# Gate rows of a chunked recurrence: loaded once and spread by VectorE shuffles, in place of repeated broadcast loads

## The chip, the cores and the metric

The kernel runs on one core of one Trainium2 chip. The metric is the device time of one execution in microseconds, from runs on the chip. The profile is one more execution, recorded by the hardware profiler.

The engines that matter here: TensorE (PE, matmuls, with PEld for its weight loads), VectorE (DVE), ScalarE (ACT), GpSimd (POOL), and SyncE (SP), which only issues transfers. Transfers between DRAM and the on-chip memory run on 16 DMA engines that all queues share. Each engine works through its own instructions in a fixed order and waits on semaphores for the others.

## The reference, cut to what matters

One encoder layer over 2048 positions of width 1024, in float32: a combined input projection, a Hyena group (long convolutions by FFT, 512 channels) beside an mLSTM group (4 heads of 128), an output projection, cross-attention into 256 memory positions, an MLP, and RMS norms between them. The change is in the mLSTM group, a recurrence over chunks, run once in each direction:

```python
F = jnp.cumsum(fc, axis=-1)
logw = F[..., :, None] - F[..., None, :] + ic[..., None, :]
logw = jnp.where(lower, logw, -jnp.inf)
log_inter = F + m[..., None]
m_t = jnp.maximum(log_inter, jnp.max(logw, axis=-1))
w = jnp.exp(logw - m_t[..., None])
inter = jnp.exp(log_inter - m_t)
s = jnp.einsum('bhtd,bhsd->bhts', qc, kc) * w
num = jnp.einsum('bhts,bhse->bhte', s, vc) + inter[..., None] * jnp.einsum('bhtd,bhde->bhte', qc, C)
den = jnp.sum(s, axis=-1) + inter * jnp.einsum('bhtd,bhd->bht', qc, n)
h = num / jnp.maximum(jnp.abs(den), jnp.exp(-m_t))[..., None]
```

For each chunk, head and direction two vectors over the position t are needed: the negated running maximum (less the gate sum), which goes into the exponent of `w`, and `inter`, which scales the queries that meet the carried state.

## The kernel before, in words

The kernel works in chunks of 128 positions, so 16 chunks, with both directions handled together. The scores are held transposed, key position s in the partitions and query position t along the columns, four heads of 128 side by side: tiles of 128 x 512.

`gates` (lines 961 to 1060) computes the gate vectors of all chunks once, with (direction, chunk, head) as 128 rows and the 128 positions as columns, and stores two such tables to DRAM as `rows` (lines 1046 and 1047): `rows[0]` holds the negated maxima, `rows[1]` the factors `inter`. Since t runs along the columns of the score tiles, a chunk's row has to stand in all 128 partitions alike. The kernel before gets that from the transfer itself: for each chunk, direction and kind one load (line 1159) reads four rows of 128 numbers, 2 KB, and writes them to each of the 128 partitions of a tile `rw`, 256 KB. Chunk 0 forward and chunk 15 backward need no `inter`, so there are 62 such loads.

`mlstm` (line 1114) is the stage around them. It first runs the rest of the backward states (`backward`, line 1096: loads `kn` and `va`, a product on POOL, matmuls L1081, updates on VectorE L1087, stores to `cbd`). Then `loads(n)` (line 1140) issues the loads of chunk n: queries `qn`, keys `kk_t`, backward state `cbn`, values `va`, and the rows. It is called for chunks 0 and 1 ahead of the loop, and for chunk n + 2 at the end of chunk n. `rw` has four buffers for each kind, so the tiles of chunk n + 2 reuse those of chunk n. The loads of chunks 0 and 1 are pinned to the written order of the program (`keep_in_program_order`), except for `va`.

`scores(n)` computes the key-query products (L1168), multiplies the `inter` rows by the queries on POOL (L1174), adds the causal mask to the maxima on POOL (L1175), takes the exponential on ScalarE (L1177), and multiplies by the products on VectorE (L1178). The loop then forms numerator and denominator on TensorE (L1206 with the values, L1208 with the carried state), the absolute value on ScalarE (L1211), `den` on VectorE (L1214, L1215), the output `y` (tile `ht`, L1219 and L1223, two buffers), the update of the forward state (L1077, L1081, L1087), the output gate on POOL (L1228), squares on ScalarE (L1234), and after every second chunk an inverse root (lines 206 to 218), the normalisation (L1241) and the stores to `ym` (L1243).

The stage is not alone. It is interleaved by generators (`weave`, `take`) with the memory projections before it and with the attention stage behind it, whose first block of 512 positions reads four chunks of `ym`. In both, weights are loaded by SP (L368, L373, L1268), split into a high and a low part by ScalarE and VectorE (L344), and used in matmuls of three parts (L339, L340, L341). A scheduler then puts each engine's instructions in order by a modelled timeline, except for what is pinned. A change in one stage can therefore move instructions of the others.

Of the kernel before, what the change touches and what calls it, by code (L numbers as in the profile page):

```python
# [10 lines left out]
F32 = mybir.dt.float32  # L11
# [122 lines left out]
class Prog:  # L134
# [931 lines left out]
    def load_v(self, sb, n):  # L1066
        t = sb.tile([128, 4, 129], F32, tag="va", name="va", bufs=2)
        vd = self.dram("vd", (L, CH)).rearrange("(n s) c -> s n c", s=128)
        self.nc.sync.dma_start(out=t[:, :, 0:128], in_=vd[:, n].rearrange("s (h d) -> s h d", h=4))
        self.nc.vector.memset(t[:, :, 128:129], 1.0)  # L1070
        return t
# [42 lines left out]
    def mlstm(self, es):  # L1114
        nc, tc, a = self.nc, self.tc, self.a
# [5 lines left out]
        rows = self.dram("rows", (2, 128, 128))  # L1121
        cbd = self.dram("cbd", (15, 128, 516))
        sb = es.enter_context(tc.tile_pool(name="m_sb", bufs=1, side="right"))
# [4 lines left out]
        for d in range(2):  # L1128
            m = sb.tile([128, 128], F32, name=f"mask{d}")
            nc.gpsimd.memset(m, 0.0)  # L1130
            s = 1 if d == 0 else -1
            nc.gpsimd.affine_select(m, m, pattern=[[s, 128]], compare_op=ALU.is_ge, fill=-1.0e30,
                                    base=0, channel_multiplier=-s)
            masks.append(m)

        for _ in self.backward(sb, 7, 0, self.old_state(sb, 8)):
            yield 3
        load, load_v, update = (partial(f, sb) for f in (self.load_c, self.load_v, self.update))

        def loads(n):  # L1140
            get = (lambda out, in_: tc.keep_in_program_order(nc.sync.dma_start(out=out, in_=in_))) if n < 2 else \
                (lambda out, in_: nc.sync.dma_start(out=out, in_=in_))
            qn = sb.tile([128, 4, 128], F32, tag="qn", name="qn", bufs=2)
            kk_t = sb.tile([128, 4, 128], F32, tag="kt", name="kk_t", bufs=2)
            get(out=qn, in_=qt[:, :, 128 * n:128 * n + 128])
            get(out=kk_t, in_=kt_[:, :, 128 * n:128 * n + 128])
            cbn = None
            if n < 15:
                cbn = sb.tile([128, 4, 129], F32, tag="cbn", name="cbn", bufs=2)
                get(out=cbn.rearrange("d h e -> d (h e)"), in_=cbd[n])  # L1150
            va = load_v(n)
            rows_ = {}
            for d in range(2):
                r = 64 * d + 4 * n
                for i in range(2):
                    if i == 1 and (n == 0, cbn is None)[d]:
                        continue
                    t = sb.tile([128, 4, 128], F32, tag=f"r{i}", name="rw", bufs=4)
                    get(out=t.rearrange("p h t -> p (h t)"),
                                      in_=rows[i, r:r + 4].rearrange("h t -> (h t)").unsqueeze(0).broadcast_to([128, 512]))  # L1160
                    rows_[d, i] = t
            return qn, kk_t, cbn, va, rows_

        def scores(n, ld):
# [4 lines left out]
            for d in range(2):  # L1169
# [8 lines left out]
                nc.vector.tensor_tensor(nm, nm, sp, ALU.mult)  # L1178

        ld, stores = [loads(0), loads(1)], []  # L1180
        scores(0, ld[0])
        cf = None
        for n in range(16):
# [10 lines left out]
            for d in range(2):  # L1194
                r = 64 * d + 4 * n
# [5 lines left out]
                for p in range(2):  # L1201
                    pn = self.hy()
                    for i in range(2):
                        h = 2 * p + i
# [11 lines left out]
                for p, pv in enumerate(pvs):  # L1216
# [4 lines left out]
                    for i in range(2):  # L1221
                        h = 2 * p + i
# [13 lines left out]
            if n % 2:  # L1236
                rv = self.bank_rsqrt(sb, ss, 128)
                for i, y in enumerate(ys):
                    t0 = 128 * (n - 1 + i)
                    for h in range(4):  # L1240
# [3 lines left out]
                        out=ym[t0:t0 + 128].rearrange("t (h e) -> t h e", h=4), in_=y))  # L1244
            if n < 14:
                ld.append(loads(n + 2))
# [713 lines left out]
```

## Time and profile before

| what | value |
|---|---|
| median of three runs | 3217.77 us (3217.51 to 3219.89) |
| profiled execution | 3216.99 us |
| its span, first to last instruction | 3215.3 us |
| mean granted TensorE clock | 0.981 |
| PE busy | 3047.5 us, 95% |
| DVE busy | 2036.0 us, 63% |
| ACT busy | 1500.1 us, 47% |
| POOL busy | 1182.7 us, 37% |
| moved by DMA | 617.87 MB, mean 192 GB/s |

How to read the lines below: a group of instructions is named by its line in the kernel (L1178 is line 1178), its engine and operation, what it writes and what it reads (`rw<-rows`), and its shapes. "Idle before" is the time in which the engine stood still just ahead of these instructions, with what ended most of it. The chain of waits is followed back from the last instruction, at each step to what released it. The granted clock is the share of TensorE's full clock that it was given. The recurrence's chunks run from about 1190 to 1640 us of the span.

### The profile page before, as it was taken

Reading aid. Unit: us, or ns where it says so; the run is one execution under the profiler, and the core shown is the slowest. Engines: PE = TensorE matmul, PEld = TensorE weight load, DVE = VectorE, ACT = ScalarE, POOL = GpSimd, SP = SyncE. Lnnn points to the kernel's source line nnn. Section 1 sums busy time; section 2 is a strip of 40 time slices with the busy share of each in tenths; the row PEclk is TensorE's granted clock in tenths of the full one; section 3 lists DMA queues with packets and bytes.
Section 4 is the critical chain, followed back from the end, with each engine's and each line's share of the span. In section 5 each row is a group of like instructions: output and inputs, shape, how many; then the busy total and the mean of one; then the engine's idle time right before and its main releaser. Section 6 shows DMA issues by size and latency. Waiting matters only on the chain.

```text
span 3215.3 us, 43642 instructions
## 1 busy us (share of the span) xinstructions
PE 3047.5 (95%) x14473; PEld 2394.2 (74%) x14473; DVE 2036.0 (63%) x3439; ACT 1500.1 (47%) x2873; POOL 1182.7 (37%) x818
## 2 busy tenths in 40 slices
PE   6999999999999976999999998999999999999998
PEld 4655566876668765878887886888788878888876
DVE  7775366345865755667775547556645676556595
ACT  5533366434764343454444445455555443333335
POOL 0122012100121334224151217776756483434483
PEclk9999999999999997999999999999999999999999
DMA  5564776686687989657484537665644474444434
GB/s 189 191 206 162 247 201 202 178 274 185 180 235 209 295 281 280 195 174 246 141 276 141 182 111 243 215 198 179 201 152 153 157 246 154 144 129 150 125 92 167
DMA packets 453817, 617.87 MB, mean 192 GB/s; under 512 B 39630, under 2 KB 251726, under 8 KB 452568
## 3 DMA queue, kind: packets, MB, share of 16 engines
q1 hardware_dynamic: 415412, 556.57, 55.2%
q10 hardware_dynamic: 38180, 58.51, 5.5%
q8 instruction: 115, 1.88, 0.2%
q14 instruction: 110, 0.90, 0.1%
HBM read 416.73 MB, written 198.21 MB: 191 GB/s over the span
## 4 chain that ended last, share of the span: by engine, by line
PE 71%; DMA 13%; DVE 8%; issue 3%; ACT 3%; POOL 1%; SPq 1%; ACTq 0%; DVEq 0%; POOLq 0%
PE mm L339 15%; PE mm L341 15%; PE mm L340 15%; PE hy L341 5%; PE hy L339 5%; PE hy L340 5%; PE hy L176 2%; DMA rw<-rows 2%; PE hy L875 1%; PE mm L844 1%; PE hy L917 1%; DVE wl L344 1%; DMA xt<-in_x_t_dram 1%; DVE bl L1533 1%; DMA va<-vd 1%
## 5 line engine op out<-in xcount | busy, mean ns | idle before, releaser
L344 DVE TENSOR_TENSOR wl<-wn,wh 128x512 fp32r<-128x512 f32 (+1 forms) x364 | 289.0, 829 | 125.5 <-ACT wh L344 124.9
L1533 DVE TENSOR_TENSOR bl<-wr,bh 128x512 fp32r<-128x512 f32 x213 | 241.1, 1138 | 126.8 <-ACT bh L1532 123.2
L1532 ACT CAST ah<-w 128x512 fp32r<-128x512 f32 x284 | 176.3, 622 | 300.1 <-PE hy L340 154.8
L344 ACT CAST wh<-wn 128x512 fp32r<-128x512 f32 (+1 forms) x364 | 207.9, 618 | 209.3 <-PE mm L341 47.8
L922 POOL TENSOR_TENSOR b<-b,a 128x512 f32<-128x512 f32 x64 | 87.7, 1370 | 581.4 <-ACT b L920 457.1
L339 PE MATMUL mm<-xh,wh 128*128 128x512 f32 x640 | 270.1, 423 | 4.5 <-ACT xh L499 2.3
L1533 DVE TENSOR_TENSOR al<-w,ah 128x512 fp32r<-128x512 f32 x236 | 222.0, 942 | 58.6 <-ACT ah L1532 58.6
L340 PE MATMUL mm<-xl,wh 128*128 128x512 f32 x640 | 256.7, 402 | 1.9 <-DVE xl L344 1.4
L341 PE MATMUL mm<-xh,wl 128*128 128x512 f32 x640 | 258.1, 404 | 0.0
L1532 ACT CAST bh<-wr 128x512 fp32r<-128x512 f32 x232 | 143.7, 621 | 240.0 <-PE mm L341 177.0
L341 PE MATMUL mm<-bh,al 128*128 128x512 f32 x576 | 225.4, 394 | 8.0 <-DVE al L1533 4.7
L339 PE MATMUL mm<-bh,ah 128*128 128x512 f32 x576 | 226.6, 393 | 0.1
L340 PE MATMUL mm<-bl,ah 128*128 128x512 f32 x576 | 225.8, 392 | 0.0
L339 PE MATMUL mm<-act,wh 128*128 128x512 f32 x512 | 199.0, 394 | 4.2 <-ACT act L344 2.7
L340 PE MATMUL mm<-act,wh 128*128 128x512 f32 x512 | 201.2, 394 | 0.0
L341 PE MATMUL mm<-act,wl 128*128 128x512 f32 x512 | 200.0, 392 | 0.3 <-DVE wl L344 0.3
L1382 POOL TENSOR_TENSOR ssum<-ssum,sq 128x512 f32<-128x512 f32 x56 | 81.1, 1448 | 287.7 <-ACT sq L1381 287.7
L339 PE MATMUL hy<-bh,ah 128*128 128x512 f32 x448 | 175.2, 391 | 0.0
L340 PE MATMUL hy<-bl,ah 128*128 128x512 f32 x448 | 174.6, 390 | 0.0
L341 PE MATMUL hy<-bh,al 128*128 128x512 f32 x448 | 174.4, 390 | 0.0
L339 PEld LDWEIGHTS mm<-xh,wh 128*128 128x128 f32 x640 | 121.1, 189 | 65.4 <-issue 29.5
L339 PE MATMUL hy<-xh,ah 128*128 128x512 f32 x384 | 152.2, 397 | 8.9 <-ACT ah L1532 8.2
(367 smaller groups left out, 8439.4 us busy)
## 6 DMA issues: line engine op xcount, KB each, us to landing
wr<-hc SPq DMA_DIRECT2D x224, 256.0 KB
w<-in_ff_w_dram SPq DMA_DIRECT2D x176, 256.0 KB
hc<-t SPq DMA_DIRECT2D x128, 256.0 KB
wn<-in_w_in_dram SPq DMA_DIRECT2D x100, 256.0 KB
hc<-q SPq DMA_DIRECT2D x96, 256.0 KB
fs<-a SPq DMA_DIRECT2D x32, 512.0 KB
a<-fs SPq DMA_DIRECT2D x64, 256.0 KB
a<-zs SPq DMA_DIRECT2D x64, 256.0 KB
```

Of the source, the lines that this page charges most:

```text
L176: b = self.nc.tensor.matmul(*products[-1], start=True, stop=True)
L339: mm(ps, lh, rh, start=start, stop=False)
L340: mm(ps, lh, rl, start=False, stop=False)
L341: mm(ps, ll, rh, start=False, stop=stop)
L344: both = (self.nc.scalar.copy(hi, src), self.nc.vector.tensor_tensor(lo, src, hi.bitcast(F32), ALU.subtract))
L844: nc.tensor.matmul(pp, dm[:, m], t[:, m], start=True, stop=True)
L875: nc.tensor.matmul(pg, em[:, m], y, start=True, stop=True)
L917: nc.tensor.matmul(pp, dm[:, m], t[:, m], start=True, stop=True)
L922: nc.gpsimd.tensor_tensor(xt, xt, hi[:, m], ALU.mult)
L1382: nc.gpsimd.tensor_tensor(ssum, ssum, sq, ALU.add)
L1532: self.nc.scalar.copy(hi, src)
L1533: eng.tensor_tensor(lo, src, hi.bitcast(F32), ALU.subtract)
```

## The change

In place of the 62 broadcast loads, the tables are loaded once into two tiles `rows0` and `rows1`, each 128 x 512. Tile s holds the rows of chunks 8s to 8s + 7, for both directions and both kinds: 2 x 2 x 8 = 32 rows of 512 numbers (four heads of 128), one to a partition. A VectorE shuffle moves data among the 32 partitions of a group only, so the same 32 rows are loaded four times, one copy to each group of 32 partitions: eight loads of 64 KB, ahead of the remaining backward states. Where `loads(n)` issued a row load on SP, it now issues a `stream_shuffle` on VectorE, whose mask names one partition for all 32 outputs: each group of 32 partitions fills with one row, and so all 128. The tiles `rw`, their number of buffers and all that reads them stay as they are. The shuffles are not pinned for chunks 0 and 1, as the loads were.

```diff
+        packed_rows = []
+        by_half = rows.rearrange("i (d s n h) t -> s (i d) n (h t)", d=2, s=2, n=8)
+        for s in range(2):
+            t = sb.tile([128, 512], F32, name=f"rows{s}")
+            for q in range(4):
+                nc.sync.dma_start(out=t[32 * q:32 * q + 32], in_=by_half[s])
+            packed_rows.append(t)
         for _ in self.backward(sb, 7, 0, self.old_state(sb, 8)):
             yield 3
...
             for d in range(2):
-                r = 64 * d + 4 * n
                 for i in range(2):
                     if i == 1 and (n == 0, cbn is None)[d]:
                         continue
                     t = sb.tile([128, 4, 128], F32, tag=f"r{i}", name="rw", bufs=4)
-                    get(out=t.rearrange("p h t -> p (h t)"),
-                                      in_=rows[i, r:r + 4].rearrange("h t -> (h t)").unsqueeze(0).broadcast_to([128, 512]))
+                    nc.vector.stream_shuffle(out=t.rearrange("p h t -> p (h t)"), in_=packed_rows[n // 8],
+                                             mask=[16 * i + 8 * d + n % 8] * 32)
                     rows_[d, i] = t
```

## The prediction, made before the result was known

> **What bounds the kernel now.** First the page's header, then the busy time of the engines by stretch (columns: PE, PEld, DVE, ACT and POOL busy with counts, granted clock, DMA share, GB/s).
>
> ```profile
> span 3215.3 us, 43642 instructions
> ```
>
> ```profile
> 1150.00:1185.00 35.00, 27.39 (x152) 22.50 (x151) 16.32 (x46) 11.41 (x21) 7.61 (x11) 0.95 0.99 311
> 1185.00:1300.00 115.00, 78.19 (x443) 68.72 (x444) 64.11 (x187) 49.40 (x171) 49.50 (x38) 0.81 0.93 288
> 1300.00:1625.00 325.00, 314.97 (x1670) 267.30 (x1669) 226.54 (x538) 156.01 (x425) 89.30 (x65) 0.99 0.58 184
> 1625.00:3215.00 1590.00, 1546.62 (x6863) 1272.93 (x6861) 1007.70 (x1350) 715.09 (x1282) 840.40 (x572) 0.99 0.53 170
> ```
>
> TensorE sets the pace nearly everywhere (97% busy from 1300 us on). The exception is 1150 to 1300 us: there the DMA engines are 93 to 99% busy, TensorE idles 44 us (7.6 and 36.8) and its clock falls to 0.81. That is where the recurrence starts, and the chain of waits through it, next, says on what.
>
> ```profile
> by line: DMA rw<-rows 32.0%; issue 10.8%; PE hy L1206 5.5%; POOL rw L1175 5.4%; DVE ht L1241 5.2%; DMA qn<-qt 5.1%; PE hy L1081 4.6%; DMA va<-vd 4.6%; ACT rw L1177 4.0%; PE hy L1208 3.7%; PE hy L1168 3.2%; PE hy L1343 2.1%; PE mm L339 1.7%;
> ...
> 1187.33 6.31 DMA rw<-rows
> 1193.65 7.97 DMA rw<-rows
> ...
> 1212.68 6.93 DMA rw<-rows
> ...
> 1227.91 5.65 DMA rw<-rows
> ...
> 1260.37 5.37 DMA rw<-rows
> ...
> 1284.40 6.14 DMA qn<-qt
> 1290.57 6.22 DMA rw<-rows
> ```
>
> This view covers 1185 to 1305 us, 120 us. Row loads hold 32% of it: the six rows sum to 38.4 us. How many loads that is, by the issues of 1185 to 1300 us and by the tile over the whole run:
>
> ```profile
> DMA packets 30429, 33.17 MB, mean 288 GB/s; under 512 B 1923, under 2 KB 19866, under 8 KB 30419
> ...
> rw<-rows SPq DMA_DIRECT2D x31, 256.0 KB
> ```
>
> ```profile
> L1142 SPq DMA_DIRECT2D rw<-rows x55: 319/423/1635, 1195.1 to 1560.4; - x55
> L1141 SPq DMA_DIRECT2D rw<-rows x7: 319/423/611, 1185.0 to 1194.3; - x7
> ```
>
> So 62 loads of 256 KB in all, 31 of them (8.13 MB of 33.17) in the bound stretch.
>
> **What the change removes.** Sixty-two loads go. Were the stretch set by DMA throughput alone, 8.13 MB at 288 GB/s is 28 us; the chain gives 38 us as the upper end. Neither is paid in full, because something else is late next each time, so I walk the places, taking TensorE's gaps with the rows that end them (in brackets: idle before, releaser).
>
> ```profile
> 1237.17 0.77 PE L1206 MATMUL hy<-va,rw 128*128 128x129 f32 x2 [5.12 <-issue]
> ...
> 1251.01 2.06 PE L1081 MATMUL hy<-ve,kn 128*128 128x129 f32 x8 [8.84 <-issue]
> ```
>
> ```profile
> 1271.14 0.77 PE L1206 MATMUL hy<-va,rw 128*128 128x129 f32 x2 [7.18 <-issue]
> ```
>
> ```profile
> 1198.87 0.70 SPq L1141 DMA_DIRECT2D qn<-qt  x1
> ...
> 1238.71 2.17 SPq L1370 DMA_DIRECT2D acc<-in_x_t_dram  x1
> 1240.97 1.37 SPq L1142 DMA_DIRECT2D rw<-rows  x1
> 1242.44 1.08 SPq L1243 DMA_DIRECT2D ym<-ht  x1
> 1243.62 0.58 SPq L1142 DMA_DIRECT2D rw<-rows  x1
> ```
>
> ```profile
> 1264.40 1.26 POOL L1228 TENSOR_TENSOR ht<-ht,og 128x512 f32<-128x512 f32 x1
> 1265.90 1.43 POOL L1175 TENSOR_TENSOR rw<-rw,mask 128x512 f32<-128x512 f32 x1 [0.24 <-DMA rw<-rows]
> ```
>
> - Start: the chain's first 14.3 us (1187.33 to 1201.62) are row loads. Next late is `qn`, issued at 1198.87, behind eight row loads (seven by L1141, the first by L1142): 2.10 MB at 288 GB/s. Gain 7.3 us.
> - The load at 1212.68 ends late, but TensorE has memory-projection matmuls then. Gain 1.5 us, an estimate.
> - Gap of 5.12 us at 1237: its chain is the load of 1227.91, mask (POOL), exp (ACT), product (DVE). With the rows there two chunks early, the earlier work on those engines remains. Gain 4.5 us.
> - Gap of 8.84 us: this one stays. The `y` buffer waits for the `ym` store of 1242.44, queued behind the `acc` loads; only two row loads leave its neighbourhood (0.52 MB, 1.8 us). Gain 1.9 us.
> - Gap of 7.18 us: the row load ends at 1265.7, yet the rsqrt chain that the product stands behind on DVE starts from POOL's 1264.40 multiply, which could have started some 2.5 us sooner. Gain 3 us.
> - 1284 to 1304: `qn` (6.14 us) becomes the wait, itself sooner by the four row loads near it (1.05 MB, 3.6 us). Gain 3 us.
>
> These come to 21.2 us. The clock adds to it, by the same view for the stretches between normalisations (L1241):
>
> ```profile
> 1203.80:1237.80 34.00, 24.24 (x153) 21.22 (x154) 19.87 (x56) 16.22 (x58) 16.79 (x13) 0.92 1.00 317
> 1237.80:1271.80 34.00, 16.29 (x98) 15.37 (x98) 16.64 (x58) 9.01 (x41) 13.01 (x10) 0.65 0.87 270
> ```
>
> The second stretch, with the long gaps, has a clock of 0.65; at the first's 0.92 its 16.29 us of TensorE work would be 11.5 us. I take half of the 4.8 us, 2.5, since TensorE isn't always the one waited for. Gain in all: 23.7 us.
>
> **What it adds.** Eight loads of 64 KB (0.52 MB, 1.7 us at 311 GB/s), once, at the head of SP's queue for this stage, and 62 shuffles on VectorE. No shuffle is in this trace; the nearest rows are a 512-column copy, the product on the same tile, and, as ends, a one-input operation from SBUF and a contended two-input one.
>
> ```profile
> L1783 DVE TENSOR_TENSOR acc<-acc 128x512 f32<-128x512 f32 x24 | 32.0, 1351 | 0.0
> ...
> L887 DVE COPY a<-hy 128x512 f32<-128x512 f32 x32 | 21.8, 687 | 36.0 <-PE hy L187 32.8 <-DMA zs<-a 3.1
> ...
> L1178 DVE TENSOR_TENSOR rw<-rw,hy 128x512 f32<-128x512 f32 x32 | 20.7, 681 | 8.1 <-PE hy L1168 4.4 <-ACT rw L1177 2.8 <-ACT hy L1211 0.8
> ...
> L250 DVE TENSOR_SCALAR b<-b 128x512 f32<-128x512 f32 x8 | 3.4, 421 | 0.0
> ```
>
> ```profile
> L1070 DVE MEMSET va<- x31: 62/62/62, 890.7 to 1559.8; 128x4 f32 x31
> ```
>
> I take the copy's 0.69 us, the row of one input moved unchanged, and 0.06 us (the smallest VectorE row) for loading a mask: 0.75 us, 46.5 us in all, between 26 us (0.421 each) and 84 us (1.351 each). The Trainium skill, "VectorE: DVE Perf Modes", section on the perf-mode tier table, gives a shuffle only the 1x speed, about 2400 ns at 2048 columns; an estimate from it at 0.96 GHz is 800 ns at 512 columns, 3 us more over all 62. No run so far shows one.
>
> In the built order, eight shuffles come in one block while memory projections and the backward states still run; about 21 fall in the bound stretch and 33 in the TensorE-bound one.
>
> - The block: 6 us, but VectorE waits for loads there:
>
> ```profile
> 1165.39 0.06 DVE L1070 MEMSET va<- 128x4 f32 x1 [4.61 <-POOL ve L1077]
> ```
>
>   Some of it and of SP's eight extra issues delays the `va` memset and the state updates behind it, and so TensorE's L1081. Cost 3 us; 0 if wholly covered, 9 with nothing covered and the loads on top. The Trainium skill, "DMA: Bandwidth & Descriptors", section on bandwidth, speaks against such small loads: 64 KB takes 0.95 us. By that the eight are 7.6 us instead of 1.7, the block's cost 9 and the net gain 6 us less; the trace has no such load to decide it.
> - Bound stretch: the shuffles wait for the last matmuls that read their buffer, and stand in pairs just ahead of the `den` maximum (L1214), which waits for the same matmuls and ACT's Abs. A pair takes 1.5 us where Abs covers some 0.6; 0.9 us times ten pairs is 9 us on `den`, which frees the product banks. Half reaches TensorE: 4.5 us (0 to 15.8, all 21).
> - From 1300 us on: 33 shuffles, 25 us, on a VectorE that is idle 98 us of 325. Much of that idle time stands exactly there:
>
> ```profile
> L1214 DVE TENSOR_TENSOR den<-hy,cols 128x4 f32<-128x4 f32 x19 | 2.9, 155 | 17.8 <-ACT hy L1211 17.7
> ```
>
>   Behind the shuffles stand weight splits (L344) that TensorE waits for. I take a tenth, 2.5 us; without the idle time all 25.
>
> Sum: 23.7 less 3, 4.5 and 2.5 is 13.7 us. The profiled execution took 3216.99 us (0.8 under the median of 3217.77): 3203 us.
>
> **Rivals.**
> 1. Hidden anyway. VectorE and the `ym` store set the cadence of two chunks, so the freed DMA time turns into other waits. For: the 8.84 us gap isn't a row load's, and VectorE's 64 us in the bound stretch grows to 80. Against: 80 is well under 115. The walk then yields the start (7.3) and half of its other gains (7 of 13.9), nothing for the clock: 14.3 less costs of 10, about 3213 us.
> 2. Slower: VectorE's queue blocks. A shuffle can't start until TensorE has read the old buffer; from 1300 us on, where TensorE is late, VectorE stands still in front of weight splits that TensorE needs next. For: formerly SP's queue stood in that wait, with only loads behind it. Against: `den`, a few instructions later in VectorE's order, waits for the same matmuls already. Sixteen pairs holding 2.5 us each cost 40 us against 16 us gained before (23.7 less 3 and 4.5): about 3241 us. It decides from 1 us a pair on.
> 3. More: the stretch is bound by throughput and latency falls for all loads. Gains reach the 28 us of DMA time and TensorE keeps full clock, another 10 us (78.19 us at 0.81 is 63, 15 us less; I take two thirds); less 5 us: about 3184 us. For: 288 GB/s at a share of 0.93. The Trainium skill, "TensorE: Matmul & The Clock Gate", Part 1, ties the clock to sustained activity; the trace agrees, 0.65 beside 0.92.
>
> **How the numbers follow.** The forecast, 3190 to 3210 us by its bounds, gets 0.50; the hidden case 0.16; slower 0.17; more 0.17. A measurement of this kernel tells about 0.2% (6.4 us) from no change. Faster: 0.50, 0.17 and a fifth of the hidden case, 0.70. Same: the rest of the hidden case, 0.13. Slower: 0.17. The range 3180 to 3224 us leaves out most of the slower case and the best end of the third, some 2 in 10.
>
> **What would show it.** Right: no rows in the chain of waits; the stretch before TensorE's steady work some 15 to 20 us shorter, with 25 MB moved and a clock above 0.85; shuffles of about 0.7 us; `ym` and `qn` among the longest waits. Wrong: shuffles over 1 us, VectorE idle in front of them, TensorE under 96% after the recurrence's start because of L344, or backward states that end later.

## The result

| | median, us | runs | ratio to before, 95% interval |
|---|---|---|---|
| before | 3219.64 (3217.51 to 3222.0) | 6 | |
| after | 3200.66 (3197.89 to 3205.33) | 6 | 0.9943 [0.993, 0.9955] |

The change makes the kernel 19.0 us faster (the median of before ahead of the prediction, 3217.77 us, is that of the first three of these six runs). The profiled execution of the changed kernel took 3198.32 us, 18.67 less than that of before, and its span is 18.7 us shorter. From here on, lines after the change are named by their number in the changed kernel: the `acc` sum of the attention stage is L1376 before and L1382 after, the values' matmuls are L1212, the mask L1181, the normalisation L1247, `den` L1220. Lines from the trace of an experiment have that kernel's own numbers.

### The profile page after: what moved, and what is told of

It reads as the page before. It is cut to its first block, busy times and chain, and to the rows that moved or that the text cites. A ratio compares the mean times of both kernels' runs of the same rounds, so it can differ in the third digit from the quotient of the medians.

```text
span 3196.6 us, 43569 instructions
## 1 busy us (share of the span) xinstructions
PE 3045.5 (95%) x14473; PEld 2394.6 (75%) x14473; DVE 2064.4 (65%) x3563; ACT 1501.3 (47%) x2873; POOL 1182.7 (37%) x818
## 4 chain that ended last, share of the span: by engine, by line
PE 50%; DVE 5%; DMA 4%; issue 2%; ACT 1%; POOL 1%; SPq 0%; DVEq 0%; ACTq 0%; POOLq 0%
PE mm L341 10%; PE mm L340 10%; PE mm L339 10%; PE hy L341 5%; PE hy L339 5%; PE hy L340 5%; DVE bl L1539 1%; DMA wr<-xs 1%; DMA sm<-hg 1%; PE hy L1212 1%; PE hy L1214 1%; DVE al L1539 1%; DVE acc L1823 0%; DVE acc L1789 0%; PE hy L1349 0%
## 5 line engine op out<-in xcount | busy, mean ns | idle before, releaser
L344 DVE TENSOR_TENSOR wl<-wn,wh 128x512 fp32r<-128x512 f32 (+1 forms) x364 | 282.4, 812 | 117.5 <-ACT wh L344 115.9
```

The costliest lines, as they stand in the source:

```text
L344: both = (self.nc.scalar.copy(hi, src), self.nc.vector.tensor_tensor(lo, src, hi.bitcast(F32), ALU.subtract))
```

## The profile after

The page's header, and the busy time by the stretches of the prediction (columns as there: PE, PEld, DVE, ACT and POOL with counts, granted clock, DMA share, GB/s), of the changed kernel:

```profile
span 3196.6 us, 43569 instructions
```

```profile
...
1185.00:1300.00 115.00, 88.10 (x514) 77.93 (x513) 84.61 (x263) 46.93 (x159) 46.94 (x36) 0.82 0.80 254
1300.00:1625.00 325.00, 323.80 (x1714) 275.27 (x1713) 251.10 (x619) 164.97 (x445) 100.21 (x73) 1.00 0.52 169
...
```

In the stretch from 1185 to 1300 us TensorE was busy for 88.10 us where it had been for 78.19 (514 matmuls in place of 443), so its idle time went from 36.8 to 26.9 us. VectorE went from 64.11 to 84.61 us. The clock was 0.82 against 0.81; in a second profile of the changed kernel (e5 below) it was 0.85. From 1300 to 1625 us TensorE's idle time fell too, from 10.0 to 1.2 us, with VectorE 24.6 us busier there. That second gain had not been forecast.

What was moved in the bound stretch, and the chain of waits through 1185 to 1305 us, after:

```profile
DMA packets 30229, 29.24 MB, mean 254 GB/s; under 512 B 1686, under 2 KB 22919, under 8 KB 30218
...
wn<-in_w_out_dram SPq DMA_DIRECT2D x12, 256.0 KB
```

```profile
by line: issue 12.5%; DMA cbn<-cbd 6.1%; DMA wn<-in_xa_wo_dram 5.5%; DVE rw L1165 5.3%; PE hy L1081 4.9%; DMA cbd<-cb 4.3%; PE mm L339 4.1%; PE mm L340 3.7%; PE mm L341 3.7%; DVE ht L1247 3.7%; POOL ht L1234 3.5%; PE hy L1349 3.4%; DVE wl L
...
1204.32 7.28 DMA cbn<-cbd
...
1220.17 1.41 DVE rw L1165 x3
...
```

The 31 row loads (8.13 MB) are gone, but the bytes fell by 3.93 MB only, from 33.17 to 29.24. Other loads moved up into the room, among them the weights of the output projection ahead of the attention, twelve where there had been eight.

Of the chain, row loads held 32.0%. Now no row load is in it. It goes through `cbn`, weights of the attention, and for 5.3% through the shuffles that took the loads' place.

The shuffles and the eight small loads, by line over the whole run (minimum, median and maximum ns of one, then first and last start):

```profile
L1165 DVE LOAD_MASK_SELECT rw<-rows x62: 3/13/18, 1162.9 to 1540.9; - x62
L1165 DVE STREAM_SHUFFLE rw<-rows x62: 720/732/755, 1162.9 to 1540.9; 128x512 f32<-128x512 f32 x62
```

```profile
L1141 SPq DMA_DIRECT2D rows<-rows x8: 598/601/749, 1154.9 to 1162.2; - x8
```

A shuffle takes 0.732 us and the load of its mask 0.013 us. The eight loads keep SP for 7.88 us, and the first shuffle waits for loads (SP's and VectorE's instructions in order of time, with start and duration):

```profile
1154.89 7.88 SPq L1141 DMA_DIRECT2D rows<-rows  x8
```

```profile
1162.93 0.01 DVE L1165 LOAD_MASK_SELECT rw<-rows  x1 [3.44 <-DMA rows<-rows]
1162.93 0.74 DVE L1165 STREAM_SHUFFLE rw<-rows 128x512 f32<-128x512 f32 x1
...
1163.57 0.74 DVE L1165 STREAM_SHUFFLE rw<-rows 128x512 f32<-128x512 f32 x1
```

The idle time ahead of a shuffle is booked on its mask load, which comes first. The second shuffle starts 0.64 us after the first, before the first one's recorded 0.74 us are over, so in a row a shuffle holds VectorE for 0.64 us.

TensorE's largest gaps in the bound stretch after the change (in brackets: idle before, releaser):

```profile
1206.15 1.13 PE L1174 MATMUL hy<-qn,kk_t 128*128 128x128 f32 x8 [1.14 <-DMA kk_t<-kt]
...
1232.52 0.77 PE L1212 MATMUL hy<-va,rw 128*128 128x129 f32 x2 [4.58 <-DVE bry L214]
...
1243.62 2.06 PE L1081 MATMUL hy<-ve,kn 128*128 128x129 f32 x8 [6.15 <-issue]
...
1263.05 0.77 PE L1212 MATMUL hy<-va,rw 128*128 128x129 f32 x2 [2.87 <-DVE bry L214]
```

The three late gaps of 5.12, 8.84 and 7.18 us have become 4.58, 6.15 and 2.87; in the second profile of the same kernel they are 3.25, 6.25 and 4.63, so a single gap is known to a microsecond or two, while the times at which the gaps end agree (1232.52, 1243.62, 1263.05 in the first; 1232.49, 1243.70, 1263.38 in the second). For the first and the last the profile names the normalisation's inverse root (`bry`, L214) as releaser. These matmuls write into one of four product banks (`hy`), and the product L1184 of the next chunk's scores, which reads such a bank, ends 0.15 us ahead of the first of them. So it is most likely this bank that they wait for; the trace doesn't name it. The product stands in VectorE's order in the middle of the inverse root. For the first gap, on VectorE:

```profile
1229.36 0.17 DVE L212 TENSOR_SCALAR hy<-brm 128x8 int32<-128x8 int32 x1 [2.80 <-ACT brm L209]
...
1231.09 1.28 DVE L1184 TENSOR_TENSOR rw<-rw,hy 128x512 f32<-128x512 f32 x2
```

The product's exponentials and key-query products had ended by 1226.2 us, almost 5 us before it ran. In its order VectorE stood still for 2.80 us, until ScalarE's `brm` behind the squares was there, and began the inverse root first. For POOL's mask, which reads the rows, the groups of the bound stretch say (before, then after):

```profile
L1175 POOL TENSOR_TENSOR rw<-rw,mask 128x512 f32<-128x512 f32 x16 | 21.4, 1336 | 50.9 <-DMA rw<-rows 47.5 <-ACT act L344 1.8 <-ACT rw L1177 1.5
```

```profile
L1181 POOL TENSOR_TENSOR rw<-rw,mask 128x512 f32<-128x512 f32 x12 | 16.3, 1360 | 36.3 <-DVE rw L1165 21.9 <-DMA ym<-ht 8.4 <-DMA qn<-qt 5.9
```

It idled 50.9 us, 47.5 of them for row loads, and still idles 36.3 us, of which the shuffles end 21.9, the `ym` store 8.4 and `qn` 5.9.

Last, where the time was gained. The first `acc` sum of the attention stage marks the end of the stretch in which the recurrence runs nearly alone (before, then after):

```profile
L1376 DVE TENSOR_TENSOR acc<-mm,acc x64: 673/690/692, 1312.6 to 1926.0; 128x512 f32<-128x512 f32 x64
```

```profile
L1382 DVE TENSOR_TENSOR acc<-mm,acc x64: 674/691/692, 1300.5 to 1907.1; 128x512 f32<-128x512 f32 x64
```

It starts 12.1 us earlier (1312.6 to 1300.5). From there to the end of the span it was 1902.7 us and is 1896.1, another 6.6. Together that is the 18.7.

## The experiments

All changes are shown against the changed kernel, unless it says otherwise. One table ahead gives what was measured: the ratio to the kernel before with its interval, the start of the first `acc` sum counted from the last store of `yh` just ahead of the stage (to leave out what differs in front of it; that store itself starts between 1150.6 and 1158.6 us), and TensorE's busy time in the 275 us from 1350 to 1625 us. The last two columns come from one profile each: the changed kernel's two agree within 0.6 us, but the profiled execution can lie well off the median of its kernel, from 6.7 us under it (e4) to 6.8 us over it (e1).

| kernel | median, us | ratio, 95% | first `acc`, us after `yh` | TensorE busy of 275 us |
|---|---|---|---|---|
| before | 3219.64 | 1 | 160.7 | 266.89 |
| after | 3200.66 | 0.9943 [0.993, 0.9955] | 149.9 | 273.80 |
| e5, after again | 3202.62 | 0.9942 [0.9929, 0.9954] | 149.6 | 274.36 |
| e2, shuffles for chunks 0 to 7 alone | 3218.67 | 0.9988 [0.9977, 0.9999] | 159.6 | 268.14 |
| e3, shuffles for chunks 8 to 15 alone | 3213.17 | 0.9978 [0.9966, 0.9989] | 166.9 | 274.23 |
| e4, before plus 62 unread shuffles | 3240.7 | 1.0053 [1.0033, 1.0074] | 176.4 | 268.18 |
| e12, after plus 62 unread shuffles | 3216.49 | 0.9985 [0.9974, 0.9996] | 163.5 | 273.63 |
| e1, after plus 62 unread loads | 3220.29 | 0.9998 [0.9986, 1.001] | 166.4 | 273.78 |
| e9, unread loads for chunks 0 to 7 | 3215.48 | 0.9983 [0.9972, 0.9993] | 164.5 | 274.32 |
| e10, unread loads for chunks 8 to 15 | 3225.76 | 1.0014 [1.0003, 1.0025] | 171.3 | 273.36 |
| e11, 62 unread loads of a quarter | 3224.28 | 1.0008 [0.9996, 1.002] | 170.6 | 273.61 |
| e6, the eight loads on ScalarE's queue | 3207.19 | 0.9956 [0.9944, 0.9969] | 152.7 | 273.30 |
| e7, the eight loads earlier | 3208.34 | 0.9963 [0.9951, 0.9976] | 152.1 | 273.75 |
| e8, four `y` buffers | 3203.61 | 0.9945 [0.9931, 0.9958] | 151.7 | 273.80 |

**The change again, and by halves.** The whole change once more:

> The full change once more, beside the runs that follow. If the two halves (first eight chunks, last eight chunks) act apart, it should gain about the sum of their two gains, 11 us, ratio 0.9966. If the halves help each other, because the order that the planner makes for the whole differs, or because row loads left in one half still hold the other up, it stays at 0.9943, 18 us.

3202.62 us, ratio 0.9942: the gain is firm. The halves give a shuffle to one half of the chunks and leave the loads to the other:

```diff
-                    nc.vector.stream_shuffle(...)
+                    if n < 8:      # the other half: n > 7
+                        nc.vector.stream_shuffle(...)
+                    else:
+                        r = 64 * d + 4 * n
+                        get(out=t..., in_=rows[i, r:r + 4]....broadcast_to([128, 512]))
```

> Shuffles for chunks 0 to 7 alone, broadcast loads for 8 to 15 (one packed tile, four small loads). My prediction priced the late shuffles at a cost of 2.5 us and the late loads at nothing: 2 to 3 us faster than the full change, about 3198 us. The changed kernel's trace speaks for a rival: TensorE's idle time from 1300 to 1625 us fell from 10.0 to 1.2 us, so the late loads cost something too; then this is 6 to 9 us slower than the full change, 3207 to 3210 us.

> The other half: broadcast loads for chunks 0 to 7, shuffles for 8 to 15. By my prediction there is nothing to gain there and 2.5 us of shuffle cost: 3219 to 3223 us. By the rival (late loads cost TensorE about 9 us): 3209 to 3213 us. If the two halves' gains sum to the whole, they act apart.

Shuffles in the first half alone gain 3.9 us (0.12% of 3221), in the second half alone 7.1, and 18.7 together (0.58%). The halves don't add up: 7.7 us are missing, a little more than the three intervals together allow (6.5 us). Both forecasts of the first half (about 3198, or 3207 to 3210 us) missed its 3218.67; the second half came as its rival said, 3209 to 3213. In the first half's trace the row loads and the bound stretch are:

```profile
L1149 SPq DMA_DIRECT2D rw<-rows x31: 320/422/650, 1328.2 to 1561.9; - x31
```

```profile
1185.00:1300.00 115.00, 81.74 (x463) 72.99 (x464) 81.05 (x232) 43.91 (x149) 45.67 (x35) 0.81 0.75 237
...
```

```profile
L1387 DVE TENSOR_TENSOR acc<-mm,acc x64: 673/688/693, 1314.1 to 1928.4; 128x512 f32<-128x512 f32 x64
```

No row is loaded before 1328.2 us, so the bound stretch has the same shuffles as after the change, four small loads fewer and 237 GB/s instead of 254. Yet TensorE is busy for 81.74 us there (463 matmuls) and not for 88.10 (514), and the first `acc` sum starts 159.6 us after the `yh` store, hardly sooner than with all loads (160.7). So the absence of row loads is not sufficient for the early gain: about 10 us (159.6 against 149.9) come with something else. What suggests itself is the order that the scheduler gave the engines, which differs from the backward states on; the order was not changed by itself, so this is an inference.

The late gain behaves otherwise. The last 275 us in the first half's trace, then in the second half's:

```profile
1350.00:1625.00 275.00, 268.14 (x1440) 227.48 (x1439) 191.15 (x469) 130.01 (x366) 74.02 (x53) 0.99 0.59 186
```

```profile
1350.00:1625.00 275.00, 274.23 (x1480) 233.85 (x1479) 209.00 (x530) 135.72 (x374) 73.80 (x54) 1.00 0.51 163
```

The table's last column splits in two groups. With row loads there (before, e2, e4) TensorE is busy 266.9 to 268.2 us. In all eleven other kernels, which have none in that time, 273.3 to 274.4, whatever they do earlier. So in all of these orders, late row loads in place of shuffles cost TensorE 5 to 7 us, and replacing them gains that. TensorE's waits in these 275 us (engine, line, releaser: total, times, longest; those of 0.2 us left out), before and then after:

```profile
PE mm L339 <- ACT act L344: 2.7, 1, 2.7
PE hy L1343 <- DMA wn<-ym: 2.3, 4, 0.8
PE hy L1206 <- DVE ht L1241: 1.6, 1, 1.6
PE hy L1454 <- DVE ht L1223: 1.2, 1, 1.2
```

```profile
PE hy L1349 <- DMA wn<-ym: 0.8, 1, 0.8
```

Four kinds of wait, of 1.2 to 2.7 us each, shrink to one of 0.8. The first and the third kind stand in the other two kernels with late loads as well (2.8 and 1.6 us in e2, 3.1 and 1.7 in e4) and are absent after the change. POOL's mask shows the rows coming late in this part too (1300 to 1625 us, before and then after):

```profile
L1175 POOL TENSOR_TENSOR rw<-rw,mask 128x512 f32<-128x512 f32 x16 | 21.5, 1346 | 120.7 <-DMA rw<-rows 120.6
```

```profile
L1181 POOL TENSOR_TENSOR rw<-rw,mask 128x512 f32<-128x512 f32 x16 | 21.5, 1342 | 93.8 <-DVE rw L1165 91.9 <-DVE den L1220 1.8
```

POOL has time to spare there, and the mask still waits for its row after the change, but 27 us less over 16 masks. Whether TensorE's waits shrank by way of the mask, or because the loads no longer share SP's queue and the DMA engines, was not separated.

**What VectorE's added work costs.** In the kernel before, with all its loads kept, a shuffle into an unread tile beside each load; and, in the changed kernel, a second unread shuffle beside each:

```diff
+                    dm = sb.tile([128, 512], F32, tag="dm", name="dm", bufs=4)
+                    nc.vector.stream_shuffle(out=dm, in_=gml, mask=[16 * i + 8 * d + n % 8] * 32)
```

```diff
+                    t2 = sb.tile([128, 512], F32, tag="t2", name="t2", bufs=2)
+                    nc.vector.stream_shuffle(out=t2, in_=packed_rows[n // 8], mask=[16 * i + 8 * d + n % 8] * 32)
```

> The kernel before with its loads kept and 62 shuffles added beside them, each into a scratch tile that nobody reads: VectorE's added work by itself, without a wait on the row loads or on the matmuls that free a row tile. By my prices for VectorE (3 for the block, 4.5 in the bound stretch, 2.5 later) up to 10 us slower, 3225 to 3230 us. If VectorE's idle time hides them: 3218 to 3222 us.

> The changed kernel with a second shuffle of the same row beside each of the 62, into a tile that nobody reads: 62 x 0.745 us, 46 us more work on VectorE, no loads. Theory 1 (VectorE's added work costs what it cost in the kernel before with the loads kept, 17 to 18 us): 3219 to 3221. Theory 2 (it cost that only where the row loads stood beside it; without them it costs what was forecast, some 7 to 10 us): 3209 to 3213. Theory 3 (it lies in idle time): under 4 us.

They cost 17.1 and 13.9 us (ratio 1.0053 against 1; 0.9985 against 0.9942, of 3221 us). The first is more than was expected (up to 10 us), the second lies between its theories (10 and 17 us). But the unread shuffles didn't stand where the change's do. In the first and in the second kernel:

```profile
L1162 DVE STREAM_SHUFFLE dm<-gml x62: 708/730/750, 1167.2 to 1236.4; 128x512 f32<-128x512 f32 x62
```

```profile
L1168 DVE STREAM_SHUFFLE t<-rows x62: 708/723/749, 1171.4 to 1257.9; 128x512 f32<-128x512 f32 x62
```

Nothing holds them back, so the scheduler put all 62 into 69 and 87 us, where the change's spread from 1162.9 to 1540.9. So these are prices for 45 us of VectorE work (62 times 0.73) in and just ahead of the bound stretch: 0.3 to 0.4 us of time for 1 us of work. Scaled by count to the 31 shuffles that the change has before 1300 us, they come to 7 to 9 us. This is an estimate from the two runs; the forecast was 7.5 (3 and 4.5).

**What the loads cost.** Unread broadcast loads beside the shuffles, in all chunks, in chunks 0 to 7, in chunks 8 to 15, and in all chunks with one row of four:

```diff
+                    # in the halves: if n < 8, or if n >= 8
+                    dm = sb.tile([128, 4, 128], F32, tag="dm", name="dm", bufs=3)
+                    r = 64 * d + 4 * n
+                    get(out=dm.rearrange("p h t -> p (h t)"),
+                        in_=rows[i, r:r + 4].rearrange("h t -> (h t)").unsqueeze(0).broadcast_to([128, 512]))
...
+                    # a quarter of the bytes, in place of the get above
+                    get(out=dm[:, 0], in_=rows[i, r].unsqueeze(0).broadcast_to([128, 128]))
```

> The changed kernel with the 62 broadcast loads put back beside the shuffles, into a scratch tile that nobody reads: same rows by shuffle, but the 16 MB of traffic and the places in SP's queue are back. Theory A (the gain is the DMA time of the removed bytes): most of it goes, 3212 to 3222 us. Theory B (the gain is that no chunk waits for its own rows any more; the bytes themselves are hidden): it stays under 3206 us.

> The changed kernel, with a broadcast load of 256 KB beside each shuffle of chunks 0 to 7 alone (31 loads), into tiles that nobody reads. With such loads in all chunks the time rose by 17.6 us (3220.3 against 3202.6). Theory A (the bytes cost where the DMA engines are 83 to 99% busy, 1185 to 1300 us): nearly all of it comes back, 13 to 18 us, 3216 to 3221. Theory B (what the loads cost lies late, in chunks 8 to 15, as the experiment with loads there and shuffles elsewhere could be read): 0 to 5 us, 3203 to 3208.

> The same with the 31 unread loads in chunks 8 to 15 alone, where DMA is some 52 to 58% busy. Theory A: 0 to 4 us, 3203 to 3207. Theory B: 10 to 17 us, 3213 to 3220. If the terms add, the two extra costs (this and that of chunks 0 to 7) sum to 17.6 us; if they don't, the planner's other order of each kernel costs or saves several us by itself.

> The changed kernel with 62 unread loads in all chunks, but of one row of 128 numbers each instead of four: 64 KB into 128 partitions, a quarter of the bytes in as many transfers. If the bytes cost, a quarter of 17.6 us: 4 to 5 us, about 3207. If the number of transfers costs (their issue on SP's queue, their place in the planner's order, the waits for a free buffer), the full 17 us: about 3219.

Against the changed kernel they cost 18.0, 13.2, 23.2 and 21.3 us, each known to some 5 us by the intervals. The first alone looked like a proof that the bytes are what counts: with them, the whole gain is gone. The others take that back. The issues of the second half's loads, of the quarter loads, and their DMA traffic in the bound stretch:

```profile
L1149 SPq DMA_DIRECT2D dm<-rows x31: 319/339/692, 1171.1 to 1265.5; - x31
```

```profile
DMA packets 34557, 29.35 MB, mean 255 GB/s; under 512 B 2337, under 2 KB 27890, under 8 KB 34547
...
dm<-rows SPq DMA_DIRECT2D x57, 64.0 KB
```

First, the loads written for chunks 8 to 15 were issued from 1171.1 to 1265.5 us. Nothing waits for an unread tile and only its three buffers hold it back, so it is loaded early, and this run does not price late loads at all, as both theories had it. Second, a quarter of the bytes (62 of 64 KB, 4.06 MB) cost as much as all of them (21.3 against 18.0 us), where a quarter or at most 17 us had been expected, with as many bytes in the bound stretch as after the change (29.35 MB against 29.24). Third, 13.2 and 23.2 do not add up to 18.0. So the cost does not go by bytes. It does not go by the number of loads alone either, since 31 cost 13.2 us issued from 1193 to 1282 us, and 23.2 issued from 1171 to 1266. What the four have in common is the place: all lose it before the first `acc` sum (164.5 to 171.3 us after `yh`, against 149.9), and from 1350 us on they are as good as the changed kernel. For the quarter loads, from 1240 to 1300 us:

```profile
1240.00:1300.00 60.00, 30.16 (x160) 27.94 (x161) 37.83 (x126) 16.62 (x66) 18.65 (x15) 0.64 0.70 215
```

```profile
1240.00:1300.00 60.00, 47.61 (x263) 42.74 (x264) 48.20 (x148) 24.84 (x90) 22.22 (x17) 0.77 0.64 197
```

(The second row is the changed kernel's.) DMA is at 0.70, far from full, and still TensorE is busy for 30.16 us there (160 matmuls) where the changed kernel is for 47.61 (263). Each of these kernels also has its own order of the matmuls on TensorE from about 1170 us on. Each also brings a wait of its own: loads on SP's queue stand until an earlier unread load has landed, for 24.6, 5.8, 8.8 and 26.0 us in all. These waits don't rank the costs (18.0, 13.2, 23.2, 21.3), and how much of each cost is this wait, and how much the order, can't be told from these runs.

**Three waits that the forecast named.** The eight small loads on ScalarE's queue; the first four right behind the store of the tables and the other four behind the backward states; and the `y` tile with four buffers, so that it need not wait for the `ym` store:

```diff
-                nc.sync.dma_start(out=t[32 * q:32 * q + 32], in_=by_half[s])
+                nc.scalar.dma_start(out=t[32 * q:32 * q + 32], in_=by_half[s])
```

```diff
 # gates, behind the stores of rows
+            for q in range(4):
+                nc.sync.dma_start(out=self.rows0[32 * q:32 * q + 32], in_=by_half[0])
 # mlstm, behind the backward states
+        for q in range(4):
+            nc.sync.dma_start(out=t[32 * q:32 * q + 32], in_=by_half[1])
```

```diff
-                    y = sb.tile([128, 4, 128], F32, tag="h0", name="ht", bufs=2)
+                    y = sb.tile([128, 4, 128], F32, tag="h0", name="ht", bufs=4)
```

> The full change with its eight small loads issued by ScalarE's queue in place of SP's. In the trace of the full change they hold SP's queue for 7.9 us (1154.9 to 1162.8), ahead of the loads of the backward states, and TensorE then stands still for 6.9 us at 1171. I priced this block at 3 us. If that price is right: 2 to 4 us faster than the full change; if the whole delay reaches the end: 6 to 8 us; if DMA time hides it: no change within 2 us.

> The full change with the first packed tile loaded right after the rows are stored, some 280 us ahead of the stage, and the second behind the backward states. The first shuffles wait for no load then. Priced as the run before this one: 2 to 4 us faster than the full change by my price of the block, no change if the block was hidden.

> The full change with four output buffers (tile ht) in place of two, so that the output of chunk n + 2 does not wait for the store of chunk n. My prediction said that this wait stays (8.84 us before; 6.15 us in the trace of the full change). If it sets the cadence of the first chunks: 4 to 6 us faster than the full change. If the chain of gate, squares, inverse root and normalisation is as late: no change within 2 us.

None is faster than the change: by their ratios 4.5, 6.8 and 1.0 us slower, where 2 to 4 us faster, or no change, had been expected of the first two. By the intervals only the 6.8 us are a difference. TensorE's gap in the backward states, after the change and with the loads on ScalarE's queue:

```profile
1171.31 3.81 PE L1081 MATMUL hy<-ve,kn 128*128 128x129 f32 x16 [6.93 <-POOL ve L1077]
```

```profile
1171.74 2.09 PE L1081 MATMUL hy<-ve,kn 128*128 128x129 f32 x8 [10.06 <-POOL ve L1077]
```

The gap grows from 6.93 to 10.06 us with the loads off SP's queue. But ScalarE has work of its own, and the eight issues stand in its way:

```profile
1160.91 11.69 ACTq L1141 DMA_DIRECT2D rows<-rows  x8
1172.64 1.14 ACT L344 CAST wh<-wn 128x512 fp32r<-128x512 f32 x2 [13.74 <-DMA rows<-rows]
```

The weight split behind them waits 13.74 us, so this run moves the delay to another engine and doesn't price SP's queue alone. The backward states, though, end sooner in it (last store to `cbd` 44.1 us after the `yh` store, against 48.5 after the change), and the first `acc` sum still starts no sooner (152.7 against 149.9 us). With the rows loaded early the gap is gone from that place, two of 3.56 and 3.99 us stand beside it (at 1165 and 1177 us), and the time isn't shorter. So the block's delay of the backward states, 3 us in the sum, hides behind other work or comes back in another place. With four `y` buffers:

```profile
1240.24 0.46 PE L1212 MATMUL hy<-va,rw 128*128 128x129 f32 x2 [4.60 <-DVE bry L214]
...
1246.79 2.06 PE L1081 MATMUL hy<-ve,kn 128*128 128x129 f32 x8 [1.59 <-ACT rw L1183]
...
1267.26 0.46 PE L1212 MATMUL hy<-va,rw 128*128 128x129 f32 x2 [2.82 <-DVE bry L214]
1271.66 0.80 PE L1212 MATMUL hy<-va,rw 128*128 128x129 f32 x2 [3.17 <-DVE ht L1247]
```

The 6.15 us gap shrinks to 1.59, so it was the `y` buffer that held TensorE there. But the median stays: the gaps behind the inverse root are as long as in the changed kernel (4.60 and 2.82 against 4.58 and 2.87), and behind the second the wait for the normalisation grows to 3.17 us, where it was 0.81.

## Why the prediction was right

The total came out near the forecast, 3203.0 against 3200.66 us, though the gain was 19.0 us and not 13.7, and the mechanism held in part: the row loads left the chain, and the wait went on to others. But the sum's two halves were off in opposite directions. By the walk, the stretch up to TensorE's steady work should have gained 16.2 us (23.7 less 3 and 4.5), and the rest lost 2.5. Measured are 12.1 and a gain of 6.6. That the errors, 4.1 us too much and 9.1 too little, partly cancel is luck.

- Start, 7.3 forecast. By the first score products it gained 4.1 (before, then after):

```profile
L1168 PE MATMUL hy<-qn,kk_t x128: 272/275/447, 1208.0 to 1581.1; 128*128 128x128 f32 x128
```

```profile
L1174 PE MATMUL hy<-qn,kk_t x128: 272/275/421, 1203.9 to 1561.3; 128*128 128x128 f32 x128
```

  The next wait there is `kk_t`, the load behind `qn` (1.14 us at 1206.15), and SP's eight extra issues lie ahead of both.
- The gap of 5.12 us, 4.5 forecast: 4.58 us are left (3.25 in the second profile), behind the inverse root. The matmul behind it starts 4.7 us earlier (1237.17 to 1232.52; 1232.49 in the second profile), hardly more than the 4.1 that the start had brought. This step failed: the rows were hardly what was late last. Before too the two products stood amid an inverse root, which began at 1233.10 us, and VectorE idled only 0.83 us ahead of the second, whose row was late:

```profile
1236.38 0.69 DVE L1178 TENSOR_TENSOR rw<-rw,hy 128x512 f32<-128x512 f32 x1 [0.83 <-ACT hy L1211]
```

  Some 0.5 us were gained here.
- The gap of 8.84 us, "this one stays", 1.9 forecast: 6.15 are left, so 2.7. Right, and with four `y` buffers it was seen that the wait is the one named and that its removal brings nothing.
- The gap of 7.18 us, 3 forecast: 2.87 are left (4.63 in the second profile). But it ends only 8.1 us earlier (1271.14 to 1263.05), of which 7.4 were there at the gap before (1251.01 to 1243.62), so 0.7 us were gained here. The gap is shorter because the same 80 matmuls ahead of it took 16.6 us in place of 13.0, at a clock of 0.71 in place of 0.79 and with more short waits.
- The clock, 2.5 forecast: 0.82 against 0.81, and 0.85 in the second profile, so no gain that stands out of the difference between two profiles, and at 0.85 the first `acc` sum starts no sooner than at 0.82 (149.6 against 149.9 us). The sign "above 0.85" didn't come, and "25 MB" was wrong: the scheduler filled the room with other loads, up to 29.24 MB.
- Shuffles, 0.75 us each with the mask: 0.745 is recorded, but in a row they start 0.64 us apart, so this size was put somewhat too high. The Trainium skill, "VectorE: DVE Perf Modes", section on the perf-mode tier table, gave 800 ns by an estimate; the trace has 732, 8% under it. Counts before the bound stretch, in it and after it: 8, 23 and 31, against 8, 21 and 33.
- The eight loads, 1.7 us by bandwidth: SP is busy 7.88 us with them (0.601 us each), and the first shuffle starts 8.0 us after the first issue. The 1.7 us were too small. The estimate of 7.6 us from the Trainium skill, "DMA: Bandwidth & Descriptors", section on bandwidth, lies by the measured 7.9 us. But the page's figure is a time of transfers and the measured one SP's time for the issues, so the agreement may be chance. The 6 us less of net gain that I had hung on it are not seen: neither another queue nor an earlier load helped, though the other queue had a cost of its own.
- Late shuffles, a cost of 2.5 forecast (0 to 25): this was the term with the wrong sign. What was forecast of VectorE held, by the groups from 1300 to 1625 us:

```profile
L1165 DVE STREAM_SHUFFLE rw<-rows 128x512 f32<-128x512 f32 x31 | 21.5, 735 | 0.0
...
L1220 DVE TENSOR_TENSOR den<-hy,cols 128x4 f32<-128x4 f32 x20 | 2.9, 146 | 3.8 <-ACT hy L1217 3.8
...
L1165 DVE LOAD_MASK_SELECT rw<-rows x31 | 0.4, 12 | 0.5 <-issue 0.5
```

  The 31 shuffles have 0.5 us of idle time in front of their mask loads, and the idle time ahead of `den` fell from 17.8 to 3.8 us: they stand where VectorE had waited. But I had booked nothing, and given no reason, for the 31 loads that leave this part. They had cost TensorE 5 to 7 us, as the two groups of kernels show.

Of the signs, rows out of the chain, shuffles of about 0.7 us, and `ym` and `qn` among the waits (8.4 and 5.9 us in front of the mask) came as said. The stretch before TensorE's steady work was to be 15 to 20 us shorter and is 12.1. Of the signs against, one came: the backward states end 3.1 us later (their last store to `cbd` 48.5 us after the `yh` store, 45.4 before).

The first rival (hidden anyway) is out: the time is 12 us below it. The second (VectorE's queue blocks) is out: 0.5 us of idle time ahead of the 31 late shuffles, where it needed 1 us a pair. The third had more gain from lower latency and clock, and its clock did not come; the extra gain lies in another place. The nearest the experiments came to the slower side is the extra shuffles: 45 us more of VectorE work packed into the bound stretch cost 14 to 17 us.

What stays open: by what way late loads cost TensorE its 5 to 7 us, and how the early gain of about 11 us divides between the loads that are gone and the order that the scheduler made without them. The first-half kernel has the one without the other and gains 1.1 us there; each kernel with 31 or 62 unread operations added has another order and loses 14 to 21 us there. A kernel with the written order held fixed was not tried.

## What to carry to other kernels

Where a scheduler sets the order, adding or removing one kind of work reorders the rest, and here that seems to be worth about as much as the work itself: halves and dummies did not add up, so price such a change as a whole, and look in the trace where a dummy really ran before you read its cost. Loads that only an engine with time to spare waits for, in a stretch with two fifths of the DMA time free, still cost the busiest engine 2% of that stretch; count the loads that leave such a stretch as a possible gain. After the removal of the longest wait, read each gap's next releaser from the trace of the changed kernel: here the rows went and the gaps that remain stand behind the inverse root and the `y` buffer. And compare when gaps end, not only how long they are: one of them lost 4.3 us of its length and 0.7 us of the time.

## What the runs showed of the hardware

- A VectorE shuffle of 128 x 512 float32 is recorded with 0.732 us (0.720 to 0.755), a little longer than the 0.687 us copy of the trace before; loading its mask takes 0.013 us, where I had taken 0.06. Shuffles in a row start 0.64 us apart.
- An issue of a 64 KB load into 32 partitions took SP 0.601 us, where the 256 KB broadcast loads into 128 partitions had a minimum of 0.319 and a median of 0.423 us. The 64 KB broadcast loads into 128 partitions (e11) had the same 0.319 and 0.423, so it is not the bytes that set it.
- The same eight issues on ScalarE's queue took 0.614 us each in the median (11.69 us from the first to the end of the last), and ScalarE's next instruction waited 13.74 us.
